# A build-time model of all engines orders the mixing stage's steps, and attention's loads go out one by one

## The chip, the cores and the metric

The kernel runs on one core of a Trainium2 chip. The metric is device time in microseconds (us) for one execution of the whole program.

## The reference

One inference step of a two-layer backbone. 128 context tokens and 512 latent tokens of 1024 features pass through each layer:

```python
h   = (x * (1 + scale1) + shift1) @ W_in      # columns split into head groups
mix = W_out([RWKV-7 (4 heads) | neighbourhood attention (4 heads) | GQA (8 query, 2 key/value heads)])
x   = LN1(alpha * x + gate1 * mix)
x   = LN2(alpha * x + gate2 * SwiGLU(x * (1 + scale2) + shift2))
```

Context tokens read context tokens only; latent tokens read all 640. RWKV-7 is a recurrent scan over the tokens, forward and backward. Neighbourhood attention (NA) adds a relative-position bias and a column mask to its scores. Everything is fp32.

## The kernel before

**Stages.** Each layer projects with `W_in`, mixes, projects with `W_out`, norms, and runs the feed-forward part. The change is about mixing: roughly 292 to 562 us of the profiled execution for the first layer and 1335 to 1616 us for the second.

**RWKV.** The scan is done in chunks of 64 tokens, as eight jobs in a layer (two heads, one direction, half of the chunks each). The jobs are counted here from 0 to 15 over both layers; 0, 1, 8 and 9 run mostly while `W_in` is still being applied, the other twelve within mixing. A job runs through one chain. `products` multiplies on PE (matmuls `FT,BK`), and the ACT queue writes the result to DRAM (`md`). POOL's queue reads it back in another layout (`BT`). `inverse` inverts the 16x16 diagonal blocks on VectorE (tiles `XB`, `tmpB`). The ACT queue writes the inverse and its transpose to DRAM (`xd`, `td`), and POOL's queue reads both back (tiles `X`, `T`). `states` begins with the matmuls `T,A`, which need `T`, and ends with five sequential state steps.

**Attention.** 30 units of two score blocks each: 6 over the context, 8 of NA (`na_pair`) and 16 of GQA (`gqa_pair`). A unit multiplies keys with queries (matmuls `ks,qs`), takes a softmax on VectorE and ScalarE (tile `prob`), transposes it on PE (`ident,prob`, then `pT`) and multiplies with the values (`pT,vw`, `pT,gv`). NA and GQA work in groups of four units, with two query tiles `qs` of 128x512 and their keys `ks` for each group. All these loads stand on SP's queue, in the order of the program: `na_bias` and `na_values` load bias and values of NA, `doubled` loads `ks` (three buffers), `stacked` loads `qs` (four buffers). `na_bias` makes 16 loads a layer in runs of 32 floats, and POOL adds the mask to each in place.

**What sets the order.** The steps are Python generators. Each yields a constant, its latency, and `weave` picks the next one by that constant and by `te.now`, a count of PE time that has been issued:

```python
t = min(self.tasks, key=lambda t: (max(t.ready - self.te.now, 0.0), t.ready))
self.te.now = max(self.te.now, t.ready)
self.step(t)
```

Nothing else is modelled: an engine other than PE, or a DMA, is there only as a yielded number. Each engine then runs its instructions in the order in which they were emitted, so a matmul that waits holds up all matmuls behind it. `weave` orders mixing; during the projections, `tick` runs those steps whose `ready` has passed.

Of the kernel before, what the change touches and what calls it, by code (L numbers as in the profile page):

```python
# [8 lines left out]
F32 = mybir.dt.float32  # L9
F32R = mybir.dt.float32r  # L10
# [6 lines left out]
P = 128  # L17
# [36 lines left out]
def bc(ap, axis, n):  # L54
    a = ap.unsqueeze(axis)
    shape = list(a.shape)
    shape[axis] = n
    return a.broadcast_to(shape)


class Tensor:

    def __init__(self, eng):
        self.eng, self.now = eng, 0.0
# [11 lines left out]
        self.eng.transpose(out, src, ident)  # L76


class Task:
    def __init__(self, gen, rank=0):  # L80
        self.gen, self.rank, self.ready = gen, rank, 0.0


class Build:
    def __init__(self, tc, I, O):
        self.tc, self.nc, self.I, self.O = tc, tc.nc, I, O

    def t(self, shape, name, dt=F32):

# [151 lines left out]

    def spawn(self, gen, rank=0):
        t = Task(gen, rank)
        t.ready = self.te.now
        self.tasks.append(t)
        return t

    def step(self, t):
        lat = next(t.gen, self)
        if lat is self:  # L250
            self.tasks.remove(t)
        else:
            t.ready = self.te.now + (lat or 0.0)

    def tick(self):

# [25 lines left out]

    def psum(self, tag):

        bufs, n = {"s2": (2, 1024), "rw": (3, 512), "pv": (1, 512)}[tag]
        return self.pp_pool.tile([P, n], F32, name="ps_" + tag, tag="ps_" + tag, bufs=bufs)

    def head_sums(self, ps, col, x, ones, starts):

# [342 lines left out]
    def rwkv_job(self, l, ft, hb, d, slot, pool):  # L632
# [121 lines left out]
        def inverse():  # L754
# [166 lines left out]
    def load_attn(self, l):  # L921
        nc, I, at = self.nc, self.I, self.at
        self.nvc = at.tile([P, 2, 256], F32, name="nvc", bufs=1)
        nc.gpsimd.dma_start(self.nvc, I["c_na_v"][l])
        self.gvc = at.tile([P, 2, P], F32, name="gvc", bufs=1)
        self.units_ = self.units(l)
        first = next(self.units_)
        self.units_ = itertools.chain([first], self.units_)
        nc.gpsimd.dma_start(self.gvc, I["c_g_v"][l])

    def na_values(self, l, ft):

        nc = self.nc
        vw = self.at.tile([P, 4, 2, P], F32, name="vw", bufs=1)
# [4 lines left out]
        return vw  # L939

    def na_bias(self, l, hd):

        nc = self.nc
        bias = self.at.tile([P, 4, 8, NA_N], F32, name="bias", bufs=2)
        for j in range(4):
            b = self.rpx[0:1]
            off = hd * 15 * 16 * (RP - 1) + PAD + 15 + NA_LO[j] - 16 * j
            nc.sync.dma_start(bias[:, j], bass.AP(tensor=b.tensor, offset=b.offset + off, ap=[[RP - 1, P], [16 * (RP - 1), 8], [1, NA_N]]))  # L948
            nc.gpsimd.tensor_tensor(bias[:, j], bias[:, j], bc(self.nmask[:, j * NA_N:(j + 1) * NA_N], 1, 8), ALU.add)
        return bias  # L950

    def stacked(self, dram, h, name, n, bufs):

# [1 line left out]
        self.nc.sync.dma_start(self.r32(t), dram[:, h * CH:(h + 1) * CH, :])  # L955
        return t

    def doubled(self, dram, h):

        t = self.at.tile([P, 2, 768], F32R, name="ks", tag="ks", bufs=3)  # L960
        for u in range(2):
            self.nc.sync.dma_start(self.r32(t[u * CH:(u + 1) * CH]), dram[:, h * CH:(h + 1) * CH, :].rearrange("a p n -> p a n"))
        return t

    def out_parts(self, dram, hi, lo):
        self.nc.sync.dma_start(dram[0], self.r32(hi))
# [131 lines left out]
            yield from unit  # L1098

    def units(self, l):  # L1100
        def load(ft):
            bias = [self.na_bias(l, 2 * ft + h) for h in range(2)]
            vw, ks = self.na_values(l, ft), [self.doubled(self.nkd[ft], h) for h in range(2)]
            return vw, [(self.stacked(self.nqd[ft], h, "qs", NLAT, 4), ks[h], bias[h]) for h in range(2)]
        vw, qk = load(0)
        for kt in range(6):
            yield self.ctx_pair(l, kt)
        for ft in range(2):
            if ft:
                vw, qk = load(ft)  # L1110
            st = {}
            for j in range(4):
                yield self.na_pair(l, ft, j, qk, vw, st)
        for kv in range(2):
            ks = self.doubled(self.gkd, kv)
            for m in range(2):
                qs = [self.stacked(self.gqd[2 * m + u], kv, "qs", NLAT, 4) for u in range(2)]
                st = {}
                for t in range(4):
                    yield self.gqa_pair(l, kv, m, t, qs, ks, st)  # L1120

    def softmax(self, ps, n, negmax, scale, sums=None):

# [70 lines left out]
    def na_pair(self, l, ft, j, qk, vw, st):  # L1194
# [5 lines left out]
        for h in range(2):  # L1200
# [10 lines left out]
            nc.vector.tensor_tensor_reduce(ps[:, 0:nw], ps[:, 0:nw], bias[:, j].rearrange("p r n -> p (r n)"), 1.0, mc, ALU.add, ALU.max, mx)  # L1211
            nm = self.tp.tile([P, 1], F32, name="nm", tag="nm", bufs=4)
            nc.vector.tensor_scalar(nm, mx, -1.0, None, ALU.mult)
            if j == h == 0:
                st["sm"] = self.tp.tile([P, 4, 2], F32, name="sms", tag="sms", bufs=2)
            pr.append(self.softmax(ps[:, 0:512], 512, nm, 1.0, st["sm"][:, j, h:h + 1]))
            yield 3.2729999999999997 if h else 0.0
        for h in range(2):
            pT.append(self.transposed(pr[h], 4))
            yield 1.091 if h else 0.0  # L1220
        if j == 0:
            st["pv"] = self.psum("pv")
        pv = st["pv"]
        for b in range(4):
# [3 lines left out]
        if j == 3:  # L1228
            o = self.out[2 + ft][0][:, NCTX:]
            yield 1.0  # L1230

            view = lambda t: t.rearrange("p (j r c) -> p j r c", j=4, r=8)
            self.normed(o.rearrange("p (r j c) -> p j r c", r=8, j=4), pv, st["sm"], view)

    def gqa_pair(self, l, kv, m, t, qs, ks, st):

# [3 lines left out]
        for h in range(2):  # L1240
# [9 lines left out]
            if t == h == 0:  # L1250
                st["sm"] = self.tp.tile([P, 4, 2], F32, name="sms", tag="sms", bufs=2)
            pr.append(self.softmax(ps[:, 0:768], 768, nm, sc, st["sm"][:, t, h:h + 1]))
            yield 3.8185 if h else 0.0
        for h in range(2):
            pT.append(self.transposed(pr[h], 6))
            yield 1.3092 if h else 0.0
        if t == 0:
            st["pv"] = self.psum("pv")
        pv = st["pv"]
        vs = slice(kv * CH, (kv + 1) * CH)  # L1260
# [4 lines left out]
        if t == 3:  # L1265
            yield 1.0
            self.normed(self.out[4 + 2 * kv + m][0][:, NCTX:], pv, st["sm"], lambda t: t)


    def gated(self, l, which, mt, c, ps, xa, z):  # L1270
# [341 lines left out]
```

## Time and profile before

| | |
|---|---|
| runs | 2167.08, 2172.19 (median), 2173.63 us |
| profiled execution | 2173.96 us, span 2172.2 us |
| PE busy | 2056.1 us (95%) |
| VectorE, ScalarE, GpSimd (POOL) busy | 60%, 42%, 12% |
| mean granted TensorE clock | 0.967 |

[...] The span runs from the first to the last instruction.

### The profile page before, as it was taken

Reading aid. Unit: us, or ns where it says so; the run is one execution under the profiler, and the core shown is the slowest. Engines: PE = TensorE matmul, PEld = TensorE weight load, DVE = VectorE, ACT = ScalarE, POOL = GpSimd, SP = SyncE. Lnnn points to the kernel's source line nnn. Section 1 sums busy time; section 2 is a strip of 40 time slices with the busy share of each in tenths; the row PEclk is TensorE's granted clock in tenths of the full one; section 3 lists DMA queues with packets and bytes.
Section 4 is the critical chain, followed back from the end, with each engine's and each line's share of the span. In section 5 each row is a group of like instructions: output and inputs, shape, how many; then the busy total and the mean of one; then the engine's idle time right before and its main releaser. Section 6 shows DMA issues by size and latency. Waiting matters only on the chain.

```text
span 2172.2 us, 41222 instructions
## 1 busy us (share of the span) xinstructions
PE 2056.1 (95%) x16737; PEld 1863.3 (86%) x16737; DVE 1304.0 (60%) x2874; ACT 909.6 (42%) x1823; POOL 250.5 (12%) x435
## 2 busy tenths in 40 slices
PE   6989989799999999999999999879999999999997
PEld 4877877577889999999989887657779999999997
DVE  6536677586776666666766567657767533233247
ACT  3434455455563212222466445546555421221234
POOL 0012242121100000000020224311101000000000
PEclk9999998899999999999999999879999999999998
DMA  8555354110414444444431415521114122222223
GB/s 296 147 155 167 108 107 91 41 44 20 153 63 142 150 145 156 146 146 144 142 133 69 134 64 106 99 55 27 32 45 138 61 74 73 72 70 84 77 84 111
DMA packets 158276, 226.48 MB, mean 104 GB/s; under 512 B 88533, under 2 KB 99413, under 8 KB 157957
## 3 DMA queue, kind: packets, MB, share of 16 engines
q1 hardware_dynamic: 118244, 200.82, 29.7%
q0 software_dynamic: 7568, 17.83, 3.0%
q10 hardware_dynamic: 32274, 5.20, 1.4%
q8 instruction: 132, 2.16, 0.4%
q14 instruction: 58, 0.48, 0.1%
HBM read 198.37 MB, written 25.40 MB: 103 GB/s over the span
## 4 chain that ended last, share of the span: by engine, by line
PE 78%; DMA 9%; DVE 5%; ACT 3%; issue 2%; SPq 1%; POOL 0%; ACTq 0%; POOLq 0%; DVEq 0%
PE ps_s L72 44%; PE ps_rw L72 26%; PE ps_pv L72 5%; PE ps_rw L76 4%; DMA td<-TB 2%; DMA qs<-nqd 2%; DMA wmod<-in_w_mod 1%; DMA T<-td 1%; SPq L948 1%; ACT whi L277 0%; DVE wlo L278 0%; SPq L938 0%; DMA xa<-in_xT 0%; DMA c_raw<-in_cT 0%; DMA vw<-vd 0%
## 5 line engine op out<-in xcount | busy, mean ns | idle before, releaser
L72 PE MATMUL ps_s<-xh,whi 128*128 128x320 f32 x1312 | 420.7, 323 | 25.2 <-ACT xh L277 11.6
L72 PE MATMUL ps_s<-xh,wlo 128*128 128x320 f32 x1312 | 412.8, 315 | 2.5 <-DVE wlo L278 2.5
L72 PE MATMUL ps_s<-xl,whi 128*128 128x320 f32 x1312 | 412.6, 315 | 0.6 <-DVE xl L278 0.4
L72 PEld LDWEIGHTS ps_s<-xh,whi 128*128 128x128 f32 x1312 | 251.6, 192 | 48.7 <-ACT xh L277 13.7
L72 PEld LDWEIGHTS ps_s<-xh,wlo 128*128 128x128 f32 x1312 | 252.1, 192 | 7.1 <-DVE wlo L278 4.4
L72 PEld LDWEIGHTS ps_s<-xl,whi 128*128 128x128 f32 x1312 | 252.4, 192 | 5.8 <-issue 2.9
L278 DVE TENSOR_TENSOR wlo<-wraw,whi 128x1024 fp32r<-128x1024 f32 (+1 forms) x118 | 141.3, 1198 | 157.5 <-ACT whi L277 157.1
L72 PE MATMUL ps_s<-xh,flo 128*128 128x320 f32 x736 | 228.4, 310 | 0.0
L72 PE MATMUL ps_s<-xl,fhi 128*128 128x320 f32 x736 | 228.3, 310 | 0.0
L72 PE MATMUL ps_s<-xh,fhi 128*128 128x320 f32 x736 | 228.3, 310 | 0.0
L277 ACT CAST whi<-wraw 128x1024 fp32r<-128x1024 f32 (+1 forms) x118 | 121.2, 1028 | 246.4 <-PE ps_s L72 144.7
L277 ACT CAST fhi<-wraw 128x1024 fp32r<-128x1024 f32 (+1 forms) x82 | 83.3, 1016 | 206.1 <-PE ps_s L72 99.5
L72 PEld LDWEIGHTS ps_s<-xh,fhi 128*128 128x128 f32 x736 | 138.7, 188 | 0.1
L72 PEld LDWEIGHTS ps_s<-xl,fhi 128*128 128x128 f32 x736 | 138.7, 188 | 0.0
L72 PEld LDWEIGHTS ps_s<-xh,flo 128*128 128x128 f32 x736 | 138.6, 188 | 0.1
L278 DVE TENSOR_TENSOR flo<-wraw,fhi 128x1024 fp32r<-128x1024 f32 (+1 forms) x82 | 96.9, 1183 | 57.8 <-ACT fhi L277 57.8
L1431 ACT ACTIVATE sg<-ps_s 128x320 f32<-128x320 f32 x88 | 38.2, 434 | 189.5 <-PE ps_s L72 189.3
L1432 DVE TENSOR_TENSOR sg<-sg,ps_s 128x320 f32<-128x320 f32 x88 | 42.7, 485 | 123.1 <-ACT sg L1431 122.5
L72 PE MATMUL ps_s<-ks,qs 128*128 128x256 f32 (+1 forms) x384 | 101.9, 370 | 11.6 <-DMA qs<-nqd 6.8
L1278 DVE SCALAR_TENSOR_TENSOR z<-ps_rw,modT,z 128x128 f32<-128x128 f32 (+2 forms) x144 | 58.9, 435 | 89.7 <-PE ps_rw L72 89.5
L1287 POOL COPY lnS<-z 128x320 f32<-128x320 f32 x8 | 6.3, 786 | 917.1 <-DVE z L1278 892.6
L72 PE MATMUL ps_rw<-hh,flo 128*128 128x320 f32 x352 | 109.1, 310 | 0.6 <-DVE flo L278 0.6
(400 smaller groups left out, 4642.4 us busy)
## 6 DMA issues: line engine op xcount, KB each, us to landing
wraw<-in_w_ffn_in SPq DMA_DIRECT2D x88, 512.0 KB
wmod<-in_w_modT SPq DMA_DIRECT2D x66, 512.0 KB
wraw<-in_w_in_f SPq DMA_DIRECT2D x42, 512.0 KB
wraw<-in_w_ffn_out SPq DMA_DIRECT2D x48, 448.0 KB
wmod<-in_w_mod SPq DMA_DIRECT2D x48, 256.0 KB
wraw<-in_w_out SPq DMA_DIRECT2D x16, 512.0 KB
wraw<-in_w_ffn_out SPq DMA_DIRECT2D x16, 512.0 KB
ks<-nkd SPq DMA_DIRECT2D x16, 384.0 KB
```

What stands on the lines that cost most here:

```text
L72: self.eng.matmul(out, lhsT, rhs, **kw)
L76: self.eng.transpose(out, src, ident)
L277: self.nc.scalar.copy(hi, src)
L278: self.nc.vector.tensor_tensor(lo, src, self.r32(hi), ALU.subtract)
L948: nc.sync.dma_start(bias[:, j], bass.AP(tensor=b.tensor, offset=b.offset + off, ap=[[RP - 1, P], [16 * (RP - 1), 8], [1, NA_N]]))
L1278: nc.vector.scalar_tensor_tensor(z[:, a:b], ps[:, q], g, xa[:, q], ALU.mult, ALU.add)
L1287: nc.gpsimd.tensor_copy(self.lnS[c], z)
L1431: nc.scalar.activation(sg, pg, AF.Silu)
L1432: nc.vector.tensor_tensor(sg, sg, pu, ALU.mult)
```

## The change

**Model and order.** A class `Model` reads every instruction as it is emitted and gives it an end on its engine or its queue, from the ends of what it reads and overwrites. `weave` now picks the task with the earliest modelled start (`start`); RWKV's tasks have 0.1 us of preference, and a change of the PE's tile shape costs 0.1 us. `tick` is as before.

**Loads.** Attention's loads are a task of their own, `loads`, with a yield after each. A group's loads are emitted when the groups named beside it in a list are done, and a unit waits until its group is loaded. The order of groups goes from NA 0, NA 1, then the four of GQA, to NA 0, two of GQA, NA 1, two of GQA. The bias comes as four loads a layer in runs of 48 floats into a tile `braw`, which shares one buffer with the NA values `vw`; POOL masks from there into eight buffers.

**A yield.** The last yield of `inverse` grows from 1.5 to 8.0.

```diff
+        elif op == "DMACopy":
+            issue = {E.SP: 0.5, E.Pool: 0.65, E.Activation: 0.3}.get(e, 0.4)
+            t = self.place(e, t, issue)
+            q = (e, "q")
+            end = self.free[q] = max(self.free.get(q, 0.0), t + 1.3) + outs[0][5] * outs[0][6] * 4 / 200e3
+            end += 0.7
+        else:
+            d = {E.DVE: (0.15, 1.04e-3), E.Activation: (0.14, 0.87e-3), E.Pool: (0.2, 2.4e-3)}.get(e, (0.1, 0.0))
+            end = self.place(e, t, d[0] + n * d[1])
...
             t.ready = self.te.now + (lat or 0.0)
+            t.due = max(m.pe if pe else t.due, end if (lat or 0.0) > 0.35 and t.rank < 3 else 0.0)
+            if t.rank == 3 or not pe and not end:
+                t.due = max(t.due, m.pe) + (lat or 0.0)
...
+        pe, mode, tags = self.known.get(t.at(), (True, None, ()))
+        if not pe:
+            return t.due, t.due
+        s = max(t.due, m.pe)
+        for tag in tags:
+            old = self.ring[tag][-self.banks[tag][0]:]
+            if len(old) == self.banks[tag][0]:
+                s = max(s, max((u[5] for u in m.used.get(old[0], ())), default=0.0))
+        return s + (0.1 if mode and mode != m.mode else 0.0) - (0.1 if t.rank < 2 else 0.0), t.due
...
-            t = min(self.tasks, key=lambda t: (max(t.ready - self.te.now, 0.0), t.ready))
+            t = min(self.tasks, key=self.start)
...
-            yield 1.5
+            yield 8.0
...
-        bias = self.at.tile([P, 4, 8, NA_N], F32, name="bias", bufs=2)
-        for j in range(4):
-            b = self.rpx[0:1]
-            off = hd * 15 * 16 * (RP - 1) + PAD + 15 + NA_LO[j] - 16 * j
-            nc.sync.dma_start(bias[:, j], bass.AP(tensor=b.tensor, offset=b.offset + off, ap=[[RP - 1, P], [16 * (RP - 1), 8], [1, NA_N]]))
-            nc.gpsimd.tensor_tensor(bias[:, j], bias[:, j], bc(self.nmask[:, j * NA_N:(j + 1) * NA_N], 1, 8), ALU.add)
-        return bias
+        if hd % 2 == 0:
+            self.braw[hd // 2] = self.at.tile([P, 2, 8, 48], F32, name="braw", tag="vw", bufs=1)
+        raw = self.braw[hd // 2][:, hd % 2]
+        b = self.rpx[0:1]
+        off = hd * 15 * 16 * (RP - 1) + PAD + 15 - 16
+        self.nc.sync.dma_start(raw, bass.AP(tensor=b.tensor, offset=b.offset + off, ap=[[RP - 1, P], [16 * (RP - 1), 8], [1, 48]]))
...
+    def na_masked(self, hd, j):
+        bias = self.bias[hd, j] = self.at.tile([P, 8, NA_N], F32, name="bias", bufs=8)
+        o = NA_LO[j] - 16 * j + 16
+        self.nc.gpsimd.tensor_tensor(bias, self.braw[hd // 2][:, hd % 2, :, o:o + NA_N], bc(self.nmask[:, j * NA_N:(j + 1) * NA_N], 1, 8), ALU.add)
...
+    def loads(self, l):
+        self.ks, self.qs, self.vw, self.braw, self.bias = {}, {}, {}, {}, {}
+        def after(*g):
+            while any(self.left[i] for i in g):
+                yield 1.0
+        def na(ft):
+            for h in range(2):
+                self.na_bias(l, 2 * ft + h)
+                yield 1.0
+            for h in range(2):
+                self.qs[ft, h] = self.stacked(self.nqd[ft], h, "qs", NLAT, 4)
+                yield 1.3
+                yield from self.doubled(self.nkd[ft], h, (0, 2 * ft + h))
+            for j in range(4):
+                for h in range(2):
+                    self.na_masked(2 * ft + h, j)
+                yield 1.6
+            yield from self.na_values(l, ft)
+        def gqa(kv, m):
+            if m == 0:
+                yield from self.doubled(self.gkd, kv, (1, kv))
+            for u in range(2):
+                self.qs[2 + 2 * kv + m, u] = self.stacked(self.gqd[2 * m + u], kv, "qs", NLAT, 4)
+                yield 1.0
+        for n, (g, need) in enumerate(((0, ()), (2, ()), (3, (0,)), (1, (0, 2)), (4, (3,)), (5, (1,)))):
+            yield from after(*need)
+            yield from na(g) if g < 2 else gqa((g - 2) // 2, g % 2)
+            self.got.add(g)
...
+        def unit(g, j, st):
+            while g not in self.got:
+                yield 0.5
+            if g < 2:
+                qk = [(self.qs[g, h], self.ks[0, 2 * g + h], self.bias[2 * g + h, j]) for h in range(2)]
+                yield from self.na_pair(l, g, j, qk, self.vw[g], st)
+            else:
+                kv, m = divmod(g - 2, 2)
+                yield from self.gqa_pair(l, kv, m, j, [self.qs[g, u] for u in range(2)], self.ks[1, kv], st)
+            self.left[g] -= 1
...
+        while self.pvs:
+            yield 0.5
```

How the instructions stand now, at three places. `order` numbers are left out; a tile's number only tells buffers apart.

SP's queue at the start of the first layer's mixing, behind the stores of `vd`, before:

```order
L1087 DMA vd_2436<-nv 64x128 x16
L948 DMA bias<-rpx_1055 128x8x32 x8
L938 DMA vw<-vd_2436 128x1x128 x8
L962 DMA ks<-nkd_1128 64x2x768 x4
L955 DMA qs<-nqd_1127 128x1x512 x2
L962 DMA ks<-nkd_1128 64x2x768 x2
L955 DMA qs<-nqd_1127 128x1x512 x2
```

and of the change:

```order
L1285 DMA vd_2414<-nv 64x128 x16
L1110 DMA braw<-rpx_1055 128x8x48 x2
L1153 DMA qs<-nqd_1127 128x1x512
L1160 DMA ks<-nkd_1128 64x2x768 x2
L1153 DMA qs<-nqd_1127 128x1x512
L1160 DMA ks<-nkd_1128 64x2x768 x2
L1099 DMA vw<-vd_2414 128x1x128 x8
L1160 DMA ks<-gkd_1571 64x2x768 x2
L1153 DMA qs<-gqd_1570 128x1x512 x3
```

The first `qs` stood behind 8 bias loads, 8 value loads and 4 key loads, and now stands behind two loads of `braw`.

PE in the second layer, up to the first `T,A` of the last job (number 15), before:

```order
L72 MATMUL ps_rw<-RV_17101,N_16920 64x64 x7
L72 MATMUL ps_s_17350<-ks,qs 128x512 x2
L72 MATMUL ps_s_17350<-ks,qs 128x256 x2
L72 MATMUL ps_rw<-RV_17101,N_16920 64x64 x3
L72 MATMUL ps_rw<-bmean,gnsq 128x2 x3
L72 MATMUL ps_s_17372<-ks,qs 128x512 x2
L72 MATMUL ps_s_17372<-ks,qs 128x256 x2
L72 MATMUL ps_rw<-T_17367,A_17050 64x64
L76 MATMUL ps_rw<-ident,prob 128x128 x6
```

and of the change:

```order
L72 MATMUL ps_rw<-S_17097,A_16919 64x64 x2
L72 MATMUL ps_rw<-RV_16860,N_16783 64x64 x10
L76 MATMUL ps_rw<-ident,prob 128x128 x6
L72 MATMUL ps_s_17238<-ks,qs 128x512 x2
L72 MATMUL ps_s_17238<-ks,qs 128x256 x2
L72 MATMUL ps_s_17284<-ks,qs 128x512 x2
L72 MATMUL ps_s_17284<-ks,qs 128x256 x2
L72 MATMUL ps_pv<-pT,gv 64x128
L72 MATMUL ps_rw<-T_17043,A_16855 64x64
L76 MATMUL ps_rw<-ident,prob 128x128 x6
```

Since the last `FT,BK` of that job, 51 rows of PE stood ahead of this `T,A` before, and 40 do now.

POOL in the second layer, from the products of job 11 to the loads of job 12's `T` and `X`, before:

```order
L679 COPY FT_15273<-FT_15273 64x5x64
L760 MEMSET XB_16057 40x256
L761 MEMSET XB_16057 40x16
L690 COPY kk_14404<-rt_15073 128x320
L876 MEMSET S_16010 128x64
L880 COPY S_16010<-st 128x64
L799 DMA X_15534<-xd_1028 64x5x64
L797 DMA T_15535<-td_1031 64x5x64 x2
```

and of the change:

```order
L840 COPY FT_15245<-FT_15245 64x5x64
L1115 TENSOR_TENSOR bias<-braw,nmask 128x256
L1037 MEMSET S_15873 128x64
L1041 COPY S_15873<-st 128x64
L1115 TENSOR_TENSOR bias<-braw,nmask 128x256 x4
L921 MEMSET XB_15942 40x256
L1115 TENSOR_TENSOR bias<-braw,nmask 128x256
L922 MEMSET XB_15942 40x16
L1115 TENSOR_TENSOR bias<-braw,nmask 128x256 x2
L851 COPY kk_14387<-rt_15122 128x320
L960 DMA X_15261<-xd_1028 64x5x64
L958 DMA T_15262<-td_1031 64x5x64 x2
```

The eight masks of the second NA group now stand directly ahead of these loads, in the first layer (job 4) as well.

## Rows read from the trace of the kernel before

**Rows 1.** Waits of PE, 290 to 620 us: us in total, times, longest.

```profile
PE ps_rw L72 <- DMA T<-td: 12.5, 4, 11.6
PE ps_s L72 <- DMA qs<-nqd: 3.9, 1, 3.9
```

**Rows 2.** The same, 1300 to 1625 us.

```profile
PE ps_rw L72 <- DMA T<-td: 15.6, 2, 8.5
PE ps_s L72 <- DMA qs<-nqd: 2.9, 1, 2.9
```

**Rows 3.** PE in order of time, three waits.

```profile
323.65 0.80 PE L72 MATMUL ps_s<-ks,qs 128*128 128x256 f32 x2 [3.91 <-DMA qs<-nqd]
...
404.24 0.44 PE L72 MATMUL ps_rw<-T,A 64*64 64x64 f32 x2 [11.60 <-DMA T<-td]
...
1459.56 0.44 PE L72 MATMUL ps_rw<-T,A 64*64 64x64 f32 x2 [8.54 <-DMA T<-td]
```

**Rows 4.** Stretches behind waits: length, busy us by engine, granted clock, DMA share, GB/s.

```profile
core 0: us, PE busy (x) PEld busy (x) DVE busy (x) ACT busy (x) POOL busy (x), PEclk, DMA share, GB/s
323.65:343.00 19.35, 18.26 (x93) 12.81 (x95) 10.43 (x43) 5.58 (x17) 0.32 (x2) 0.50 0.13 46
404.24:415.00 10.76, 10.76 (x82) 7.88 (x83) 4.09 (x9) 3.67 (x8) 0.45 (x1) 0.51 0.04 9
...
1365.20:1405.00 39.80, 34.26 (x297) 27.67 (x296) 26.66 (x98) 19.07 (x48) 8.41 (x12) 0.83 0.45 78
1415.70:1425.00 9.30, 9.29 (x124) 7.84 (x124) 4.24 (x11) 3.07 (x7) 0.45 (x1) 0.68 0.19 60
1459.55:1466.00 6.45, 6.44 (x82) 5.55 (x84) 2.10 (x5) 2.48 (x5) 1.44 (x4) 0.50 0.05 15
1466.00:1600.00 134.00, 133.35 (x1593) 105.42 (x1592) 100.00 (x268) 78.15 (x163) 23.04 (x33) 1.00 0.11 28
```

**Rows 5.** ACT's queue: the writes of `td` of jobs 4, 5, 12 and 15.

```profile
385.27 0.28 ACTq L793 DMA_DIRECT2D td<-TB  x1
...
440.55 0.29 ACTq L793 DMA_DIRECT2D td<-TB  x1
...
1443.05 0.28 ACTq L793 DMA_DIRECT2D td<-TB  x1
...
1584.68 0.28 ACTq L793 DMA_DIRECT2D td<-TB  x1
```

**Rows 6.** POOL: the loads of `T` of the same four jobs.

```profile
401.50 1.35 POOL L797 DMA_DIRECT2D T<-td  x2 [2.77 <-DMA td<-TB]
...
451.27 0.69 POOL L797 DMA_DIRECT2D T<-td  x1 [10.86 <-DMA td<-TB]
...
1456.66 1.33 POOL L797 DMA_DIRECT2D T<-td  x2 [1.70 <-DMA td<-TB]
...
1587.34 1.33 POOL L797 DMA_DIRECT2D T<-td  x2
```

**Rows 7.** SP's queue: loads of `qs`.

```profile
385.56 0.51 SPq L955 DMA_DIRECT2D qs<-gqd  x1
...
439.56 2.24 SPq L955 DMA_DIRECT2D qs<-gqd  x2
...
1442.78 0.52 SPq L955 DMA_DIRECT2D qs<-gqd  x1
```

**Rows 8.** DMA rate, 360 to 406 us in 40 equal slices.

```profile
GB/s 185 270 222 214 213 138 73 75 103 73 74 81 48 57 50 48 48 50 50 48 134 255 216 165 86 50 48 49 27 29 39 48 48 48 109 11 0 103 110 1
```

**Rows 9.** SP's queue as the first layer's mixing begins.

```profile
290.21 8.32 SPq L948 DMA_DIRECT2D bias<-rpx  x8
298.57 4.81 SPq L938 DMA_DIRECT2D vw<-vd  x8
...
308.07 2.50 SPq L955 DMA_DIRECT2D qs<-nqd  x2
```

**Rows 10.** POOL: three masks.

```profile
359.28 2.21 POOL L949 TENSOR_TENSOR bias<-bias,nmask 128x256 f32<-128x256 f32 x3 [0.34 <-DMA bias<-rpx]
```

**Rows 11.** PE by kind and shape, 1466 to 1600 us: count, busy us, mean ns.

```profile
L76 PE MATMUL ps_rw<-ident,prob 128*128 128x128 f32 x180 | 27.0, 280 | 0.5 <-DVE RV L838 0.5
```

**Rows 12.** PE: the last `FT,BK` of job 15.

```profile
1562.62 0.71 PE L72 MATMUL ps_rw<-FT,BK 64*128 64x128 f32 x4
```

**Rows 13.** Tile `T`, 1300 to 1625 us: issue of its loads to their landing.

```profile
DMA to landing us min/median/max: 2.4/2.7/6.0
```

More of the change, by code (lines that the diff above doesn't have):

```diff
@@ L76, in transpose, with __init__, __contains__, region @@
         self.eng.transpose(out, src, ident)
+class Names:
+    def __init__(self, *dicts):
+        self.names = {d[k][tuple([slice(0, 1)] * len(d[k].shape))].tensor.name for d in dicts for k in d}
+        self.scratch = ("nqd", "nkd", "gqd", "gkd", "vd", "rpx", "md", "td", "xd", "xres")
+    def __contains__(self, name):
+        return name in self.names or name.rstrip("0123456789_") in self.scratch
+class Model:
+    def __init__(self, nc):
+        self.nc, self.n, self.block, self.pe, self.mode = nc, 0, None, 0.0, None
+        self.free, self.gaps, self.used, self.before = {}, {}, {}, {}
+    def region(self, arg):
+        a = getattr(arg, "bass_ap", None)
+        if a is None:
+            return None
+        dims = [list(d) for d in a.ap]
+        name, n = a.tensor.name, 1
+        for _, c in dims[1:]:
+            n *= c
+        if name in self.nc_dram:
+            lo = a.offset + sum(min(0, s * (c - 1)) for s, c in dims)
+            hi = a.offset + sum(max(0, s * (c - 1)) for s, c in dims) + 1
+            return name, 0, 1, lo, hi, n, dims[0][1]
+        pitch = max(dims[0][0], 1)
+        p, f = divmod(a.offset, pitch)
+        lo = f + sum(min(0, s * (c - 1)) for s, c in dims[1:])
+        hi = f + sum(max(0, s * (c - 1)) for s, c in dims[1:]) + 1
+        return name, p, p + dims[0][1], lo, hi, n, dims[0][1]
+    def last(self, r, writes):
+        name, p0, p1, f0, f1 = r[:5]
+        if name not in self.used:
+            self.used[name] = []
+            old = self.used.get(self.before.get(name), ())
+            return max((u[5] for u in old), default=0.0) if not writes else 0.0
+        return max((u[5] for u in self.used[name] if (u[0] or not writes) and u[1] < p1 and p0 < u[2] and u[3] < f1 and f0 < u[4]), default=0.0)
+    def place(self, e, t, d):
+        g = self.gaps.setdefault(e, [])
+        i = len(g)
+        while i and g[i - 1][0] > t:
+            i -= 1
+        if i and g[i - 1][1] > t:
+            t = g[i - 1][1]
+        while i < len(g) and g[i][0] < t + d:
+            t = max(t, g[i][1])
+            i += 1
+        g.insert(i, (t, t + d))
+        del g[:-60]
+        return t + d
+    def add(self, ins):
+        e, op = ins.engine, ins.opcode
+        outs = [r for r in map(self.region, ins.outs) if r]
+        inp = [r for r in map(self.region, ins.ins) if r]
+        if not outs:
+            return None
+        t = max([self.last(r, True) for r in inp] + [self.last(r, False) for r in outs]) + 0.07
+        n = max(r[5] for r in outs + inp)
+        E = mybir.EngineType
+        pe = False
+        if op == "Matmult":
+            pe = True
+            k, m = inp[1][6], inp[1][5]
+            n = inp[0][5]
+            mode = (128 if k > CH else CH, 128 if m > CH else CH)
+            if ins.ins[0].bass_ap.dtype == F32R:
+                d = max(n * 0.458e-3, 0.06)
+            elif ins.is_transpose:
+                d = max(n, m) / 1200
+            else:
+                d = 2 * max(n * 0.883e-3, m / 1200)
+            d *= (mode[0] / 128) * (mode[1] / 128) * (1.25 if mode != (128, 128) else 1.0)
+            if mode != self.mode:
+                d += 0.1
+                self.mode = mode
+            self.pe = max(self.pe, t) + d
+            end = self.pe + 0.15
+        elif op == "DMACopy":
[7 more added lines that the diff above has]
+            end = self.place(e, t, d[0] + n * d[1])
+        for w, rs in ((True, outs), (False, inp)):
+            for r in rs:
+                u = self.used.setdefault(r[0], [])
+                u.append((w,) + r[1:5] + (end,))
+                del u[:-48]
+        return pe, op == "DMACopy" and outs[0][0] in self.nc_dram, end
+    def read(self):
+        bb = self.nc.cur_bb.bb
+        if bb is not self.block:
+            self.block, self.n = bb, 0
+        new, self.n = bb.instructions[self.n:], len(bb.instructions)
+        got = [g for g in map(self.add, new) if g]
+        return any(g[0] for g in got), max((g[2] for g in got if not g[1]), default=0.0)
@@ L79, with at @@
 class Task:
     def __init__(self, gen, rank=0):
-        self.gen, self.rank, self.ready = gen, rank, 0.0
+        self.gen, self.rank, self.ready, self.due = gen, rank, 0.0, 0.0
+    def at(self):
+        g = self.gen
+        while getattr(g, "gi_yieldfrom", None) is not None and hasattr(g.gi_yieldfrom, "gi_frame"):
+            g = g.gi_yieldfrom
+        f = getattr(g, "gi_frame", None)
+        return (f.f_code.co_name, f.f_lineno) if f else None
 class Build:
@@ L86, in __init__ @@
         self.tc, self.nc, self.I, self.O = tc, tc.nc, I, O
+        self.banks = {"s2": (2, 1024), "rw": (3, 512), "pv": (1, 512)}
+        self.ring, self.tags, self.known = {k: [] for k in self.banks}, [], {}
+        self.model = Model(self.nc)
+        self.model.nc_dram = Names(I, O)
     def t(self, shape, name, dt=F32):
@@ L243, in spawn @@
         t = Task(gen, rank)
-        t.ready = self.te.now
+        t.ready, t.due = self.te.now, self.model.pe
         self.tasks.append(t)
@@ L248, in step @@
     def step(self, t):
+        m = self.model
+        m.read()
+        at, self.tags, mode = t.at(), [], m.mode
+        m.mode = None
         lat = next(t.gen, self)
+        first = self.first_mode()
+        m.mode = mode
+        pe, end = m.read()
+        self.known[at] = (pe, first, tuple(self.tags))
         if lat is self:
@@ L283, in psum @@
     def psum(self, tag):
-        bufs, n = {"s2": (2, 1024), "rw": (3, 512), "pv": (1, 512)}[tag]
-        return self.pp_pool.tile([P, n], F32, name="ps_" + tag, tag="ps_" + tag, bufs=bufs)
+        bufs, n = self.banks[tag]
+        t = self.pp_pool.tile([P, n], F32, name="ps_" + tag, tag="ps_" + tag, bufs=bufs)
+        ring, name = self.ring[tag], t[:, 0:1].tensor.name
+        if len(ring) >= bufs:
+            self.model.before[name] = ring[-bufs]
+        ring.append(name)
+        self.tags.append(tag)
+        return t
     def head_sums(self, ps, col, x, ones, starts):
@@ L925, in load_attn @@
         self.gvc = at.tile([P, 2, P], F32, name="gvc", bufs=1)
+        nc.gpsimd.dma_start(self.gvc, I["c_g_v"][l])
+        self.left, self.got, self.pvs = [4] * 6, set(), set()
         self.units_ = self.units(l)
-        first = next(self.units_)
-        self.units_ = itertools.chain([first], self.units_)
-        nc.gpsimd.dma_start(self.gvc, I["c_g_v"][l])
+        self.loader = self.spawn(self.loads(l), 3)
     def na_values(self, l, ft):
         nc = self.nc
-        vw = self.at.tile([P, 4, 2, P], F32, name="vw", bufs=1)
+        vw = self.vw[ft] = self.at.tile([P, 4, 2, P], F32, name="vw", tag="vw", bufs=1)
         vr = self.vd.rearrange("(r c) f -> r c f", c=64)[:, :, ft * P:(ft + 1) * P]
@@ L956, in stacked, with doubled @@
         return t
-    def doubled(self, dram, h):
-        t = self.at.tile([P, 2, 768], F32R, name="ks", tag="ks", bufs=3)
+    def doubled(self, dram, h, key):
+        t = self.ks[key] = self.at.tile([P, 2, 768], F32R, name="ks", tag="ks", bufs=3)
         for u in range(2):
             self.nc.sync.dma_start(self.r32(t[u * CH:(u + 1) * CH]), dram[:, h * CH:(h + 1) * CH, :].rearrange("a p n -> p a n"))
-        return t
+            yield 2.0
     def out_parts(self, dram, hi, lo):
@@ L1220, in na_pair @@
             yield 1.091 if h else 0.0
+        while self.pvs if j == 0 else "pv" not in st:
+            yield 0.5
         if j == 0:
+            self.pvs.add(ft)
             st["pv"] = self.psum("pv")
@@ L1256, in gqa_pair @@
             yield 1.3092 if h else 0.0
+        while self.pvs if t == 0 else "pv" not in st:
+            yield 0.5
         if t == 0:
+            self.pvs.add((kv, m))
             st["pv"] = self.psum("pv")
```

38 lines of the change are left out of this document (17 added, 21 removed).

## The prediction

> **What bounds the kernel now.** PE. Outside mixing it is nearly always busy at the full clock; what can be had is PE's waits within mixing and the half clock behind them. So I read the waits of PE over both mixing stages first, then the granted clock just behind the longest of them, then the queues that the awaited data came through. Two tiles carry most of the waiting: `T`, the inverse that an RWKV job reads back from DRAM, 12.5 us in the first layer [rows 1] and 15.6 in the second [rows 2], and `qs`, the queries of the first neighbourhood group, 3.9 and 2.9 us. That is 28.1 and 6.8 us.
>
> A wait is paid for twice. Behind the 3.91 us for `qs` [rows 3] the next 19.35 us ran at a granted clock of 0.50, a loss of 9.7 us (length times one minus the clock). Behind the long waits for `T` the losses are 10.76 x 0.49 = 5.3, 9.30 x 0.32 = 3.0 and 6.45 x 0.50 = 3.2 us, together 11.5, or 3.8 for each. Behind the `qs` wait of the second layer 39.80 x 0.17 = 6.8 us are lost, of which I count half, 3.4, since other waits lie in that stretch. From 1466 to 1600 us the clock stays at 1.00 and PE is busy for 133.35 of 134 us, so the same mixture of work needs no wait [rows 4].
>
> Why `T` is late is seen on the queues. In job 15 `td` is written at 1584.68 [rows 5] and POOL loads `T` at 1587.34 [rows 6]: 2.7 us. In jobs 4, 5 and 12 the same takes 16.2, 10.7 and 13.6 us. Each of these three writes was issued within 1 us of a load of `qs` on SP's queue [rows 7]. The DMA engines were far from full: while such loads run, the rate has a plateau at 48 to 50 GB/s, a fifth of what the same window reaches elsewhere [rows 8]. A `qs` tile is 256 KB, so one takes some 5.3 us there and a pair 10.6. I conclude that a `td` issued beside a pair of `qs` loads waits for them, however little is moving.
>
> [...]
>
> **The first loads.** Before, the first `qs` went out at 308.07, behind eight bias loads that hold SP's queue for 8.32 us and eight loads of values for 4.81 [rows 9]. Now it stands behind two loads of `braw`, with as many runs each as one of the eight, and each run half again as long; at 8.32 / 8 = 1.04 us a load, or 1.56 if longer runs cost in proportion, it goes out at 292 to 294, some 14 us earlier, while the first matmul that uses it stands at the same place in PE's order within 2 us. 14 us cover the 3.9 and 2.9 us of wait. What goes: 6.8 us, and the half clock behind, 9.7 + 3.4. Together **-19.9 us**. The bound on the other side is nothing, if another operand comes as late as `qs` did; the keys go out right behind it, so I take the whole.
>
> **The order of the steps.** PE's instructions are the same before and after, so only waits can change. What matters for `T` is how much other PE work stands between a job's last `FT,BK` and its first `T,A`. I laid PE's order of both kernels end to end, each matmul at busy time over count of its kind in the stretch that has no waits (for `ident,prob` 27.0 us over 180 [rows 11]), all scaled by 0.825, because ends overlap and the groups of that view sum to 161.7 us in 133.35 [rows 4]. This estimate gives, in us of cover:
>
> Jobs 2 to 7: before 43.9, 26.0, 32.9, 31.9, 37.4, 31.3; now 35.6, 29.6, 27.6, 27.3, 26.1, 28.0.
> Jobs 10 to 15: before 37.0, 24.2, 37.3, 33.2, 33.8, 28.0; now 23.8, 25.3, 29.8, 30.8, 30.5, 22.0.
>
> An undisturbed chain needs 27 us: in job 15 the last products end at 1563.3 [rows 12], the second load of `T` goes out at 1588.0 [rows 6] and lands in 2.4 to 2.7 us [rows 13]. So the model places `T,A` about where an undisturbed chain ends. Other waits, some 10 us in a stage of 270, stretch the cover by 4%.
>
> Where nothing disturbs, three jobs are short: 10, 11 and 15, by 27 less 24.8, 26.3 and 22.9, or 2.2 + 0.7 + 4.1 = 7.0 us, and 3.8 of half clock for the last. That is a floor of 10.8 us. It would be nothing if the chain were 4 us shorter than in job 15.
>
> Each job that is disturbed adds more. The three late ones above were 13.6, 8.1 and 11.0 us later than job 15. A job can be hit by a pair of `qs` loads for anything from nothing to 13.6, and I take the middle of 2.7 and 13.6, 8.2; less some 2 us that the cover leaves, 6.2, and 3.8 of half clock, makes 10.0 us for a hit. The model does not see it: it lets a load run at 200 GB/s, 1.3 us for a `qs` where the trace shows 5.3, and gives SP's and ACT's queues no effect on each other. `qs` goes out when its buffer comes free, at the end of a group. In PE's order now, laid out as above, a pair comes free 2 us or less beside the `td` of job 3, 5 us ahead of that of job 11 and beside that of job 13 (a `td` is placed 21 us behind the last `FT,BK`, as in job 15). Pairs that fall on the products of jobs 4, 12 and 14 are sheltered, as the stall of the job ahead adds to their cover. So I take three hits: 30 us.
>
> Sum for `T`: before 28.1 + 11.5 = 39.6; now 10.8 + 30 = 40.8: **+1.2 us**. For h hits it is 10.8 + 10.0 h - 39.6; the bounds are no hit, -28.8, and seven, +41.2.
>
> **Masks on POOL.** There are 16 a layer at 0.73 us as before [rows 10], but the second NA group's eight now stand directly ahead of the `T` loads of jobs 4 and 12: 5.8 us, behind a `braw` that waits for a pair of `qs` and for `vw`'s buffer. By the laid-out order `T` lands within 1 us of its `T,A` either way. I take nothing, as both jobs have a stall ahead in their cover; without that, up to 3 us each. Queued behind the masks are these loads alone, then the products' copies.
>
> **The rest.** Softmax waits (2.3 and 2.4 us for `prob`), the state steps and the end of mixing look alike in both orders; the larger yield moves the states of jobs 0, 8 and 9 later, where PE has the projection to do. Nothing, within 3 us.
>
> Sum: -19.9 + 1.2 = -18.7 us on 2174.0 for the profiled execution (its span of 2172.2 and 1.8 around it): **2155 us**. The median of the runs shown lies 1.8 below the profiled one, which I leave out.
>
> **The rivals.** *Nothing disturbs.* The model's order happens to keep every `td` away from the pairs, at most one hit: -48.7 to -38.7, 2125 to 2135 us. For it speaks that pairs go out at fixed points now; against it that in the kernel before three of twelve jobs were hit within 1 us.
>
> *No change.* Five hits: -19.9 + 21.2 = +1.3, 2175 us. All that the first loads give back goes to waits for `T`.
>
> *Slower.* The zero slack decides: six or seven of the twelve jobs are hit, jobs 4 and 12 by the masks among them. +11.3 to +21.3, 2185 to 2195 us. It decides from five hits on. For it: the covers now, of which none from job 3 on is above 31 us, where before eight were; twelve `qs` a layer at 5.3 us are on the way for 64 of some 255 us, and a job has DMAs out at its `md` and `BT` too. Against it: a stall of one job is cover for the next.
>
> [...]
>
> **How the numbers follow.** About 6.5 us (0.3%) is what a measurement of this kernel can tell from no change. The forecast, two to four hits (2145 to 2165 us): 0.44. Nothing disturbs: 0.14. No change: 0.18. Slower: 0.24. Faster is the first two, 0.58. The range leaves one in ten out on each side: 2124 to 2188, from no hit to some six. The forecast's own range is 2145 to 2165.
>
> **What would show it.** Right: no wait for `qs` at the start of mixing and a clock of 1.00 in the 20 us behind it; waits for `T` as several of 3 to 9 us in place of one of 11.6 and two of 7 to 9; in each of them `td` out within a few us of a pair of `qs`; job 15 short by some 4 us without one. Wrong: waits for `T` under 10 us in total (the chain is shorter, or the pairs miss), over 45 us (the slack was worth more than the first loads), or a new operand at the start of mixing, `ks` or `bias`, that PE waits for.

## The result, and the profile after

The changed kernel takes 2203.2 us (2200.62 to 2204.98, 4 runs) against 2172.47 us before: the ratio is 1.0145, with a 95% interval of 1.0126 to 1.0165. It is 31 us slower. The forecast was 2155 us, and its range ended at 2188.

Where the time went is seen first in a table by stretch. These rows hold the two mixing stages, before and after: length, busy time by engine, granted clock, DMA share, GB/s.

Before:

```profile
262.00:578.00 316.00, 288.48 (x3319) 230.25 (x3319) 220.63 (x637) 173.88 (x403) 74.71 (x107) 0.94 0.29 67
1310.00:1636.00 326.00, 294.10 (x3295) 235.37 (x3295) 223.83 (x638) 172.91 (x403) 73.60 (x111) 0.92 0.28 62
```

After:

```profile
256.00:590.00 334.00, 291.17 (x3280) 230.82 (x3277) 218.03 (x635) 173.83 (x404) 69.76 (x103) 0.90 0.21 50
1321.00:1658.00 337.00, 290.90 (x3337) 231.67 (x3337) 226.68 (x658) 177.09 (x411) 72.71 (x109) 0.93 0.24 56
```

PE is busy for 582.6 us before and 582.1 after. Together the two stretches grew from 642 to 671 us (the whole span grew by 26.6), so all 29 us are PE's idle time. Work at half clock counts longer in the busy time (after, twenty `T,A` take 1.33 us at a clock of 0.50 and 0.80 at 1.00), so half clock costs about what it did; the granted clock in the table is a mean that counts idle time too (after, 302 to 313 us, PE is idle throughout and the view gives 0.63). The busy time of each other engine stays within 6 us. The waits of PE over the same two stretches after, largest first (us in total, times, longest), stand against [rows 1, 2]:

```profile
PE ps_rw L72 <- DMA T<-td: 12.4, 1, 12.4
PE ps_s L72 <- ACT prob L1322: 6.6, 8, 3.9
PE ps_rw L72 <- ACT N L989: 4.2, 1, 4.2
PE ps_s L72 <- ACT whi L432: 3.4, 1, 3.4
PE ps_rw L76 <- DVE RHO L1024: 3.3, 1, 3.3
...
PE ps_rw L72 <- DMA T<-td: 13.9, 7, 5.3
PE ps_rw L76 <- DVE RV L905: 6.5, 2, 6.2
PE ps_rw L72 <- DVE nm L1450: 4.6, 3, 2.3
PE ps_pv L72 <- DVE pT L1350: 4.0, 3, 3.3
PE ps_s L72 <- ACT whi L432: 3.4, 1, 3.4
```

Before, the largest rows for other engines were, in the first stretch and then in the second:

```profile
PE ps_s L72 <- ACT prob L1127: 2.3, 3, 1.0
PE ps_rw L72 <- DVE RV L838: 1.6, 1, 1.6
...
PE ps_s L72 <- ACT prob L1127: 2.4, 4, 1.3
PE ps_rw L72 <- DVE pT L1155: 2.3, 1, 2.3
PE ps_s L72 <- ACT vf L1077: 1.8, 1, 1.8
PE ps_s L72 <- ACT whi L277: 1.6, 1, 1.6
```

`qs` has left the list, and `T` went from 28.1 to 26.3 us. Together these two fell by 8.6 us. But the waits for VectorE, ScalarE and GpSimd, summed over all rows of both views, grew from 23.9 to 61.4 us, by 37.5. The two changes add up to the 29 us.

The largest of these new waits have one thing in common. These are three of them on PE:

```profile
343.78 0.47 PE L76 MATMUL ps_rw<-ident,prob 128*128 128x128 f32 x1 [3.28 <-DVE RHO L1024]
...
389.55 0.81 PE L72 MATMUL ps_rw<-X,N 64*64 64x64 f32 x20 [4.19 <-ACT N L989]
...
1356.99 0.96 PE L76 MATMUL ps_rw<-ident,BK 64*128 64x64 f32 x10 [6.18 <-DVE RV L905]
```

And VectorE just before each:

```profile
342.72 0.16 DVE L936 COPY XB<-BT 40x2 f32<-40x2 f32 x1 [4.96 <-DMA BT<-md]
...
387.98 0.16 DVE L936 COPY XB<-BT 40x2 f32<-40x2 f32 x1 [4.83 <-DMA BT<-md]
388.06 0.49 DVE L844 TENSOR_TENSOR BK<-rt,rt 128x320 f32<-128x320 f32 x1
...
1354.30 0.48 DVE L936 COPY XB<-BT 40x2 f32<-40x2 f32 x1 [6.67 <-DMA BT<-md]
```

VectorE stood at the first copy of an inverse (`XB` from `BT`), whose data was still on its way, with everything behind it queued. Such a wait at the copy is called a stand below. In the second case ScalarE waited for `BK`, which VectorE wrote only after that copy, and PE for what ScalarE had queued behind it. The releaser that PE's row names (ScalarE, `N`) is two steps from the cause. VectorE's own waits show the total, before and then after (two stages each):

```profile
DVE XB L775 <- DMA BT<-md: 7.7, 2, 6.7
...
DVE XB L775 <- DMA BT<-md: 4.5, 1, 4.5
```

```profile
DVE XB L936 <- DMA BT<-md: 15.5, 4, 5.0
...
DVE XB L936 <- DMA BT<-md: 17.4, 4, 6.7
```

From 12.2 to 32.9 us. Five PE waits of over 3 us, 20.9 us in all (the three above, one of 3.87 and one of 3.35), fall in such a stand.

The first `qs` loads did go out early. SP's queue, ACT's queue, POOL and PE, after, at the start of the first mixing stage:

```profile
284.01 1.01 SPq L1110 DMA_DIRECT2D braw<-rpx  x2
285.06 0.60 SPq L1153 DMA_DIRECT2D qs<-nqd  x1
...
287.43 0.68 SPq L1153 DMA_DIRECT2D qs<-nqd  x1
...
287.75 0.70 ACTq L954 DMA_DIRECT2D td<-TB  x1
...
310.93 1.34 POOL L958 DMA_DIRECT2D T<-td  x2 [7.68 <-DMA td<-TB]
...
313.63 1.75 PE L72 MATMUL ps_rw<-T,A 64*64 64x64 f32 x19 [12.41 <-DMA T<-td]
```

They now lie beside the `td` of job 2, which takes 23.2 us to reach its load (2.7 in job 15 before, [rows 5, 6]). PE waits 12.41 us there.

### The profile page after: what moved, and what is told of

Its sections match the earlier page's. It is cut to its first block, busy times and chain, and to the rows that moved or that the text cites. A ratio compares the mean times of both kernels' runs of the same rounds, so it can differ in the third digit from the quotient of the medians.

```text
span 2198.8 us, 41202 instructions
## 1 busy us (share of the span) xinstructions
PE 2055.5 (93%) x16737; PEld 1866.2 (85%) x16737; DVE 1299.2 (59%) x2874; ACT 913.7 (42%) x1826; POOL 243.7 (11%) x435
## 4 chain that ended last, share of the span: by engine, by line
PE 81%; DMA 7%; DVE 5%; ACT 4%; issue 2%; POOL 1%; ACTq 0%; POOLq 0%; SPq 0%; DVEq 0%
PE ps_s L72 44%; PE ps_rw L72 28%; PE ps_pv L72 5%; PE ps_rw L76 3%; DMA td<-TB 1%; DMA BT<-md 1%; DMA T<-td 1%; DMA md<-X 1%; ACT whi L432 1%; DMA wmod<-in_w_mod 1%; ACT xh L432 1%; ACT prob L1322 1%; DVE nm L1449 0%; DMA c_raw<-in_cT 0%; DVE tmpB L939 0%
## 5 line engine op out<-in xcount | busy, mean ns | idle before, releaser
L72 PE MATMUL ps_rw<-hh,wlo 128*128 128x320 f32 x352 | 108.8, 309 | 0.1
```

The costliest lines, as they stand in the source:

```text
L72: self.eng.matmul(out, lhsT, rhs, **kw)
```

## The experiments

Times are medians; each ratio is to the kernel before, run beside it. Sixteen kernels ran.

**Split loads.** Each `qs` load of 128 rows becomes two of 64 rows.

```diff
-        self.nc.sync.dma_start(self.r32(t), dram[:, h * CH:(h + 1) * CH, :])
+        for u in range(2):
+            self.nc.sync.dma_start(self.r32(t[u * CH:(u + 1) * CH]), dram[u, h * CH:(h + 1) * CH, :])
```

In the changed kernel. 

> The changed kernel, with each query tile qs loaded as two DMAs of 64 rows instead of one DMA over a DRAM view with slowest dimension 2. Theory A (loads of qs make BT and td late, and everything else follows from that): PE's waits for T fall from 26.3 us to under 8, VectorE's waits for BT from 32.9 to about 12, time 2140 to 2165. Theory B (the new order itself puts work too early, whatever the loads do): the waits for T go with their half clock, but PE's waits for VectorE and ScalarE stay at some 45 us, time 2170 to 2180. Rival C (qs has nothing to do with it): 2198 to 2208.

In the kernel before. 

> The kernel before, with the same split of the qs loads. If a pair of qs loads makes td late, its waits for T and qs of 34.9 us fall under 10 and the half clock behind them goes: 2115 to 2135. If td was late for another reason: 2165 to 2175.

The changed kernel took 2164.84 us (0.9959, with an interval of 0.9943 to 0.9976), the kernel before 2132.09 us (0.9810, 0.9772 to 0.9848). The split is worth 38 and 40 us, and the distance between the two kernels stays at 33. The `td` of job 2 in the changed kernel is written at 287.71 (287.75 without the split), and reaches its load in 8.6 us in place of 23.2:

```profile
296.33 1.34 POOL L958 DMA_DIRECT2D T<-td  x2 [2.09 <-DMA td<-TB]
```

PE's waits for `T` over both stages in the changed kernel, split:

```profile
PE ps_rw L72 <- DMA T<-td: 5.2, 5, 1.3
```

In the kernel before, split, PE has no row for `T` or `qs` at all. So the slow `qs` loads are what made `T` late in both kernels, and they are not what makes the changed one slower. 2165 lies at the edge between A and B. Theory A holds of `T` and of the copy, at which VectorE now waits 12.9 us in place of 32.9. Theory B holds of PE's waits for the other engines: they fell only from 61.4 to 49.1 us, though most of the stands are gone.

**A later copy out of `BT`.** An empty step at the head of `inverse`.

```diff
         def inverse():
 
+            yield 5.0
             BT = J.BT
```

> The changed kernel, with one step more at the head of the inverse that emits nothing and is due 5 us later, so that the first copy out of BT is emitted some 5 us later and other VectorE work stands ahead of it. Theory A2 (VectorE, which runs in order, stands at that copy until BT has landed, and PE waits for what is queued behind it): VectorE's waits for BT fall from 32.9 us to under 15, PE's waits for VectorE and ScalarE by some 15 to 20, time 2180 to 2192. Rival (the waits for VectorE are from other causes): the chain to T is only made longer, waits for T rise, 2200 to 2215.

2172.77 us (0.9997, 0.9978 to 1.0015): 30 of the 31 us come back, more than expected. VectorE's row for the copy and PE's for `T`:

```profile
DVE XB L937 <- DMA BT<-md: 17.6, 6, 10.7
...
PE ps_rw L72 <- DMA T<-td: 8.7, 6, 3.4
```

One stand of 10.7 us is left. But PE's waits for other engines fell only by 8.6 us, to 52.8, where 15 to 20 were expected. Its waits for `T` fell by 17.6, as all that follows the copy comes later too, and its busy time over the whole execution by 10. So it is not shown that the stand was the larger part of what came back.

**Only `T,A` later.** The same empty step at the head of `states`.

```diff
+            yield 5.0
             bmm(N, lambda k, c, h: RV[k, c, h, :], CH, ...
```

> The changed kernel with an empty step of 5 us at the head of states, so that T,A comes later (covers of jobs 3 to 7 and 10 to 15 some 5 us longer in the order) and the copy out of BT stays where it is. The later copy out of BT gave 30 us back, but it lengthened the covers of T too, and PE's waits for T fell there from 26.3 to 8.7 us. If that was the whole effect: 2168 to 2180 here as well, waits for T under 10 us. If VectorE's place at the copy was part of it: waits for T under 10, but VectorE's waits for BT stay near 33 us, 2182 to 2195.

2202.03 us (1.0104, 1.0049 to 1.0158): no gain that can be told, as its four runs lie between 2187 and 2209. The waits for `T` fell only to 15.8 us:

```profile
PE ps_rw L72 <- DMA T<-td: 15.8, 10, 6.5
PE ps_rw L72 <- DVE gnr L774: 8.8, 3, 6.3
```

Neither expectation came true: VectorE's waits at the copy did not stay near 33 us but fell to 22.0, and PE was busy for 11 us longer in the profiled execution. The order of everything else moved in both runs, so this one doesn't settle whether the copy's place or the later `T,A` brought the 30 us.

**Both mends.**

> The changed kernel with both mends, the split qs loads (38 us alone) and the later copy out of BT (30 us alone). If the two are separate causes, the gains add for the most part: 2130 to 2145, VectorE's waits for BT under 8 us and PE's for T under 8. If the second only made good what the late qs loads did to BT: no better than the split alone, 2158 to 2170.

> The kernel before with both mends. Its VectorE waited for BT for 12.5 us, and for 8.9 with the split loads alone, so there is little to gain there and the chain to T gets longer by 5 us of PE time: 2125 to 2140, about as with the split alone (2132). If the copy's place matters as much here as in the changed kernel: 2105 to 2120.

2153.04 us (0.9904, 0.9876 to 0.9932) and 2162.30 us (0.9939, 0.9901 to 0.9977). In the changed kernel 12 us come on top of the split, in the middle between the two expectations: the causes overlap, as `BT` is late partly through `qs` (32.9 to 12.9 us with the split alone). In the kernel before the same step costs 30 us over the split alone, against both expectations. An 8.7 us wait for `ks` appears there, and the empty step means another thing under the old key, which counts it in PE time; which of the two made the 30 us is open.

**The parts of the change, one by one.** The old key in `weave` with all else of the change:

```diff
-            t = min(self.tasks, key=self.start)
+            t = min(self.tasks, key=lambda t: (max(t.ready - self.te.now, 0.0), t.ready))
```

> The changed kernel with the key of the kernel before in weave (yielded numbers and counted PE time), its loads one by one and its order of groups kept. If the order given by the model costs the 31 us: 2165 to 2180. If the loads cost it: the wait of 12.4 us for T of job 2 stays, 2190 to 2205. A gain over before (under 2165) would say that the loads alone were worth having.

The yield alone, in the kernel before (`yield 1.5` to `yield 8.0`):

> The kernel before with only the last yield of the inverse changed from 1.5 to 8.0. Theory: it moves the first T,A of a job by some 6 us of PE time, which gives slack to jobs that are hit: 2160 to 2172. Rival (it leaves PE short of other work between): 2175 to 2190.

The yield back at 1.5 in the changed kernel:

> The changed kernel with the last yield of the inverse back at 1.5. In the kernel before, 8.0 in its place cost some 41 us. If the yield costs the changed kernel as much (it acts on the jobs that run during the projections): 2160 to 2175. If the model's order makes the number nearly idle: 2195 to 2208.

Loads and groups alone (old key, yield 1.5), the same with split `qs`, and the new key alone (loads, groups and yield of before):

> Only the loads one by one and the order of groups, with the old key of weave and the yield of 1.5. With the yield of 8.0 the same took 2175. If the loads are worth what their earlier qs promised and the yield costs some 30 to 40: 2135 to 2150. If loads and yield cancel nothing: 2170 to 2180.

> The loads one by one with the old key, yield 1.5, and the qs loads split. Against the kernel before with the split loads (2132): if the new loads still help, 2115 to 2128; if the split took all that they could give, 2128 to 2140.

> Only the model's order: the new key of weave on the loads and groups of before, yield 1.5. If the order alone costs the 31 us, whatever the loads: 2195 to 2215, VectorE's waits for BT near 30 us. If it costs only together with the new loads: 2165 to 2180.

| key | loads | last yield | us | ratio, interval | us, `qs` split |
|---|---|---|---|---|---|
| old | old | 1.5 (before) | 2172.5 | 1 | 2132.1 |
| old | old | 8.0 | 2215.9 | 1.0172, 1.0138 to 1.0207 | |
| old | new | 1.5 | 2206.7 | 1.0154, 1.0119 to 1.0189 | 2168.8 (0.9989, 0.9973 to 1.0006) |
| old | new | 8.0 | 2175.5 | 1.0014, 0.9994 to 1.0034 | |
| new | old | 1.5 | 2195.8 | 1.0106, 1.0062 to 1.0149 | 2168.6 |
| new | new | 1.5 | 2200.8 | 1.0141, 1.0108 to 1.0174 | |
| new | new | 8.0 (changed) | 2203.2 | 1.0145, 1.0126 to 1.0165 | 2164.8 |

The parts don't add. Each of the three alone costs 23 to 37 us by its ratio. Under the old key the new loads and the yield nearly cancel. Under the new key the yield hardly counts. I had expected the yield alone to give slack and the loads alone to gain, and both lost. Of the six rows below the first none is faster and one is level, and with the split the two that hold one part are as slow as the whole. With the loads alone VectorE stands at the copy as in the changed kernel, for 33.2 us:

```profile
DVE XB L936 <- DMA BT<-md: 33.2, 9, 9.0
```

**The new key with split loads.**

> The model's order alone (loads, groups and yield of before) with split qs loads. Against the kernel before with the same split (2132): if the model's order costs by itself, with no late qs in play, 2150 to 2170; if it cost only through the late loads, 2128 to 2138.

2168.61 us (0.9983, 0.9966 to 1.0000), 37 us above the kernel before with the same split. The order by the model costs this much with split `qs` loads. Only half of it is waiting. These are the busy times over the whole execution, the kernel before with split loads first (span 2129.0 us), then with the new key (2171.7):

```profile
PE 2040.7 (96%) x16737; PEld 1851.6 (87%) x16737; DVE 1305.1 (61%) x2874; ACT 908.9 (43%) x1823; POOL 249.5 (12%) x435
...
PE 2061.8 (95%) x16737; PEld 1869.5 (86%) x16737; DVE 1296.7 (60%) x2874; ACT 910.9 (42%) x1824; POOL 250.9 (12%) x435
```

PE's matmuls are the same in number and take 21 us longer, at a mean granted clock of 0.962 in place of 0.979; PE's idle time grew by 22.

**Mending the model.** Engines that take their work in order of emission, in place of filling gaps:

```diff
         i = len(g)
+        t = max(t, g[-1][1]) if g else t
```

> The changed kernel, with a model in which an engine takes its work in the order of emission, in place of filling gaps that lie earlier. If the gap filling hides from the model that VectorE stands at the copy out of BT and holds up the rest, the order gets better: 2170 to 2190, VectorE's waits for BT under 25 us. If the model's order fails for another reason (latencies of DMA, the moment of emission): 2195 to 2215.

`qs` loads as the trace shows them:

```diff
+            one = inp[0][0].rstrip("0123456789_") in ("nqd", "gqd")
+            t = self.place(e, max(t, self.pe) if one else t, issue)
...
+            if one:
+                self.free["qs"] = end
+            else:
+                end = max(end, self.free.get("qs", 0.0))
```

(and 50e3 in place of 200e3 for these loads).

> The changed kernel, with a model that knows the qs loads as the trace shows them: begun not before they are emitted, 50 GB/s, and other DMAs ending no earlier than they do. If the model's blindness for these loads is what puts T,A and the copy out of BT too early: waits for T and for VectorE at that copy fall by 20 us, 2165 to 2185. If its order costs for other reasons: 2195 to 2210.

More distance between a result and its reader, with split loads (0.07 to 0.3 in `add`):

> The changed kernel with split qs loads (2165) and 0.30 us in place of 0.07 between a result and its reader in the model, which leaves PE more distance behind VectorE and ScalarE. If the waits left there (48.9 us against 31.2 with the split in the kernel before) come from too little distance: 2140 to 2155. If distance is not what is missing: 2160 to 2175.

2213.54 us (1.0168, 1.0147 to 1.0189), 2204.20 us (1.0146, 1.0122 to 1.0171) and 2170.72 us (0.9991, 0.9972 to 1.0009). None of these mends of the model brought a gain by itself, which speaks against gap filling, unseen late loads and too little distance as the one cause.

**The waits side by side.** PE's waits in us over both mixing stages, VectorE's at the copy over the same, and PE's busy time over the whole execution, all from the profiled execution of each kernel:

| kernel | median us | for `T` and `qs` | for other engines | VectorE at the copy | PE busy |
|---|---|---|---|---|---|
| before | 2172.5 | 34.9 | 23.9 | 12.2 | 2056.1 |
| before, split | 2132.1 | 0 | 31.1 | 6.9 | 2040.7 |
| before, split, new key | 2168.6 | 5.9 | 48.6 | 10.6 | 2061.8 |
| changed | 2203.2 | 26.3 | 61.4 | 32.9 | 2055.5 |
| changed, split | 2164.8 | 5.2 | 49.1 | 12.9 | 2049.1 |
| changed, later copy | 2172.8 | 8.7 | 52.8 | 14.5 | 2045.4 |
| changed, both | 2153.0 | 0 | 53.2 | 9.1 | 2038.6 |
| changed, later `T,A` | 2202.0 | 15.8 | 62.3 | 22.0 | 2066.4 |

In every row with the new key PE waits 48 us or more for the other engines, with or without the stands.

## Why the prediction was wrong

In the forecast's own terms, without the rest: the waits for `T` and `qs` were to fall by 9.3 us and fell by 8.6; the half clock was to give back 9.4 (13.1 behind `qs`, less 3.7 more behind `T`), and PE's busy time fell by 0.5.

**The first loads: half right.** They went out 23 us earlier than before (the forecast said 14), 6 of them because SP's queue came to the stage's loads earlier, and PE's wait for `qs` is gone. But the 19.9 us were not gained: the loads moved onto the `td` of job 2, and its 12.41 us, with 36.37 us at a granted clock of 0.69 behind it, took their place. The forecast had named this bound (another operand as late as `qs`) and set it aside.

```profile
313.63:350.00 36.37, 30.61 (x308) 23.86 (x308) 22.53 (x86) 14.69 (x48) 8.21 (x14) 0.69 0.25 59
```

I had counted the pairs that come free at the end of a group and not the pair whose time I moved myself; job 2's cover of 35.6 us made it look safe.

**Waits for `T`: right in size, partly by luck.** The forecast's waits without their half clock were 7.0 and three times 6.2, 25.6 us. Measured: 26.3. That the slow `qs` loads make `td` late is shown by the two split runs: PE's waits for `T` and `qs` went from 34.9 us to none in the kernel before, and from 26.3 to 5.2 in the changed one. Which jobs were hit I had wrong: 2 and 10 in place of 3, 11 and 13, two waits of 12.4 and 7.1 us in place of three of 6.2. The `td` of job 10 went out 17 us behind the last `qs` load, with loads of values on SP's queue; it took 10.2 us to reach its load, and 4.1 in the changed kernel with split loads. Job 11 waited 2.4, with its `td` on time. Job 15, which I put at 4.1 us short, waited 1.25.

**The masks: not nothing.** In job 12 POOL was in the masks until 1459.5 us, loaded `T` 7.5 us behind its `td`, and PE waited 2.65 us, near the 3 that the forecast gave as a bound. In job 4 `T` went out 3.0 us behind its `td` and PE did not wait.

**The rest: the step that failed.** The forecast gave "Softmax waits (2.3 and 2.4 us for `prob`), the state steps and the end of mixing look alike in both orders" and "Nothing, within 3 us". In its place the waits for the other engines grew by 37.5 us, more than the whole loss. I had laid out PE's order alone, as PE is the bound, and looked at the other engines' busy time, which did not change. What changed is where their instructions stand in order. 20.9 us of the waits after fall where VectorE stands at the copy out of `BT`. Some 5 us of the growth are at the ends of mixing: PE now waits 3.4 us in each layer for the `whi` of `W_out`, before 1.6 and 0.2; that attention ends last and leaves nothing beside it is my reading. Seven further waits of 1.0 to 2.4 us, 10.9 in all, fall where VectorE was busy for 10.6. But taking the stands away does not take their 20.9 us away: with the split or the later copy, VectorE's time at the copy fell by 20 and 18 us, and PE's waits for other engines by 12 and 9. What else in the order makes PE wait is not shown.

**The rival on the other side** was right in its sign and wrong in its cause. It put the loss on more hits of `T` (six or seven); there were two (jobs 2 and 10), and the time passed its 2195.

**Why a `td` beside `qs` loads is late.** The forecast drew it from a plateau of 48 to 50 GB/s [rows 8] and three late jobs, and the runs agree as far as they go: the same bytes in two loads over 64 rows brought the `td` of job 2 to its load in 8.6 us in place of 23.2. By what mechanism a load over 128 rows is slow, and holds up a small write of another queue, no run shows.

**What stays open.** The stand at the copy out of `BT` is a cause that the trace shows for five waits. Moving the copy (with all behind it) recovers 30 us, more of it in the waits for `T` and in busy time than in those for other engines. And 37 us of the new key remain with split loads, where VectorE waits 10.6 us at that copy; half of them are PE's matmuls taking longer, which the forecast counted only behind waits for `T` and `qs`. Three mends of the model left the time where it was or made it longer. Since each part of the change alone costs 23 to 37 us and they don't add, I take it that the order before was tuned as a whole and that any large move away from it costs some 30 us; that is argued, not shown.

The best kernel of the study is the one before with split `qs` loads: 2132 us, 1.9% under before and 3.2% under the changed one.

## What to carry to other kernels

Lay out the order of every engine that PE waits for, not PE's alone: here a copy on VectorE stood for 6.67 us at its DMA and held up what was queued behind it, PE waited 6.18 us for that, and VectorE's busy time in the two stages shows nothing of it (444.5 us before, 444.7 after). When a transfer is moved, list what else is on the queues at its new time. And the slow transfer was better mended here at its shape than scheduled around: two lines in place of one were worth 40 us, and a new scheduler with its loads cost 31. Last, a wait that is traced to a cause need not go when the cause does: run the kernel without the cause, and count the waits again.

## What was not expected of the hardware

Two loads of 256 KB, each over a DRAM view of 2x64x512, lay beside a small write that another engine issued within 1 us of the second. With them, and with other loads on the queues, the write took 23.2 us to reach its reader in job 2 of the changed kernel, against 2.7 in job 15 before [rows 5, 6]. For some 10 of the 23 us the rate lay at 50 GB/s or less, as in [rows 8]. The same bytes as loads of 64 rows left 8.6 us there, and no wait of PE for `T` or `qs` in the kernel before.
